# First load in one piece, and the last sixteen rows in five pieces: a row-wise ReLU sum

## The chip, the cores and the metric

The kernel runs on one core of one Trainium2 chip. The metric is device time in microseconds (us) for one execution; the time before is the median of three runs. The profile is one execution recorded by the hardware profiler, and its own time, the span, is somewhat shorter than the run time, because it starts with the first recorded instruction and ends with the last.

## The reference

```python
def setup_inputs():
    batch, seq, dim = 32, 512, 1024
    return {"x": np.random.randn(batch, seq, dim).astype(np.float32)}

def reference(x: np.ndarray) -> np.ndarray:
    relu_x = np.maximum(x, 0)
    return np.sum(relu_x, axis=-1).astype(np.float32)
```

There are 32 x 512 = 16384 rows of 1024 fp32 numbers, 64 MB (67.1 million bytes) in all. Each row gives one number: the sum of its positive elements. The output is 64 KB.

## The kernel before

**Rows on partitions.** Each of the 128 partitions handles J = 128 rows. `REGIONS = [1, 111, 16]` (line 8) cuts the input, in order of address, into three blocks. In the first block partition p holds one row, so that the block is 512 KB of consecutive memory; in the second it holds 111 consecutive rows (neighbouring partitions start 444 KB apart); in the third it holds 16 (64 KB apart). `xv` and `ov` (lines 45 to 49) are the views of input and output by block.

**Staging.** `buf` is a ring of NB = 3 buffers of 16 rows for each partition. `CHUNKS` (line 9) lists seven chunks of 16 rows. Chunk 0 comes in two loads, the single row of the first block (4 KB for each partition) and 15 rows of the second block (60 KB); chunks 1 to 6 are one load each of 64 KB for each partition. All loads go through SyncE's queue (SP), issued in the loop of line 85; chunk c waits until VectorE (DVE) has finished chunk c - 3 (line 87). Both loads of chunk 0 are moved in the instruction list ahead of SP's arrival at the start barrier (lines 79 to 84 and 95 to 97).

**The two engines.** For chunks 0 to 5 (`NTWO` of them, loop of line 138), ScalarE (ACT) does the ReLU in place over several rows at once (line 145), DVE sums the rows of each step (line 160), and in the later chunks some rows are done whole by one engine. "Whole" means one instruction that does ReLU and sum: `on_act` (line 127), which the profile shows as ACTIVATE and a read of the accumulator, or `on_dve` (line 130), shown as TENSOR_SCALAR_CACHE_REDUCE and a read of the accumulator. For chunk 6 and everything behind it, rows go alternately to DVE and ACT, whole (lines 173 to 185). `res` holds the results, one column for each of a partition's 128 rows.

**The transposed store.** The results of the first block lie in column 0 of `res`, one number for each partition. DVE transposes 32 columns of `res` in 32 x 32 squares after chunk 1 (lines 167 to 169), so that four partitions of `turned` hold the 128 numbers, and SP stores these four runs of 128 bytes (line 117), behind the last loads in its queue.

**The last 16 rows.** They come in seven loads: `TAIL = [8, 4, 2]` whole rows (line 101), and the last two rows, seen as one run of 2048 elements, in four pieces: elements 0 to 912 (`first`), 1536 to 2048 (`second`), 1280 to 1536 (`third`), in that order (line 112), and last 912 to 1280 into the tile `seam` (line 115). This last piece lies across the border of the two rows. Each earlier piece gives a partial sum (`first` two, one on each engine), which is written into `seam` right beside the loaded elements: two numbers ahead of them and two behind. Then ACT sums the 114 numbers that belong to the second-last row, and DVE the 258 of the last row (lines 199 to 203). The partial sums are not negative, so a ReLU over them changes nothing. `s_half` and `s_seam` count the partial sums and the load; `s_last` counts the two final sums.

**The stores.** The results of the second block are stored (line 123) when both engines have finished chunk 6 and the load of `third` has landed; those of the third block (line 207) after `s_last`. The program ends when the stores have landed.

Of the kernel before, what the change touches and what calls it, by code (L numbers as in the profile page):

```python
# [3 lines left out]
P = 128  # L4
D = 1024
BIG = 16
NB = 3
REGIONS = [1, 111, 16]
CHUNKS = [[(0, 0, 1), (1, 0, 15)]] + [[(1, 16 * c + 15, 16)] for c in range(6)]
ACT_STEPS = [[16], [7, 9], [7, 9], [7, 9], [4, 5, 7], [3, 4, 5]]  # L10
DVE_STEPS = [[4, 5, 7], [7, 4, 5], [7, 4, 5], [7, 4, 5], [4, 5, 7], [3, 4, 5]]
TAIL = [8, 4, 2]
CUT = 912
HEAD = 256


def bass_relu_sum_kernel(
    nc: bass.Bass,
    x: bass.AP,
    out: bass.AP,  # L20
):

    fp32 = mybir.dt.float32
    ALU = mybir.AluOpType
    AF = mybir.ActivationFunctionType
    X = mybir.AxisListType.X

    B, S, _ = x.shape
    J = B * S // P
    NBIG = len(CHUNKS)
    assert BIG * NBIG + sum(TAIL) + 2 == J == sum(REGIONS)  # L40

    xr = x.rearrange("b s d -> (b s) d")
    of = out.rearrange("b s -> (b s)")
    start = [sum(REGIONS[:i]) for i in range(len(REGIONS))]
    xv = [
        xr[P * s : P * (s + n), :].rearrange("(p j) d -> p j d", p=P)
        for s, n in zip(start, REGIONS)
    ]
    ov = [of[P * s : P * (s + n)].rearrange("(p j) -> p j", p=P) for s, n in zip(start, REGIONS)]

    buf = nc.alloc_sbuf_tensor("buf", [P, NB, BIG, D], fp32)
    w = D - CUT
    seam = nc.alloc_sbuf_tensor("seam", [P, 2 + w + HEAD + 2], fp32)
    res = nc.alloc_sbuf_tensor("res", [P, J], fp32)
    turned = nc.alloc_sbuf_tensor("turned", [P, 32], fp32)

    n_in = NBIG + len(TAIL) + 3
    s_in = [nc.alloc_semaphore(f"s_in{i}") for i in range(n_in)]
    s_act = nc.alloc_semaphore("s_act")
    s_dve = nc.alloc_semaphore("s_dve")  # L60
    s_fact = nc.alloc_semaphore("s_fact")
    s_fdve = nc.alloc_semaphore("s_fdve")
    s_half = nc.alloc_semaphore("s_half")
    s_seam = nc.alloc_semaphore("s_seam")
    s_last = nc.alloc_semaphore("s_last")
    s_turn = nc.alloc_semaphore("s_turn")
    s_store = nc.alloc_semaphore("s_store")
    s_out = nc.alloc_semaphore("s_out")

    sp, act, dve = nc.sync, nc.scalar, nc.vector  # L70

    NTWO = len(ACT_STEPS)
    done = [sum(map(len, DVE_STEPS[: c + 1])) for c in range(NTWO)]


    tb = NBIG % NB


    code = nc.main_func.blocks[0].instructions
    arrival = next(  # L80
        i
        for i, ins in enumerate(code)
        if ins.engine == mybir.EngineType.SP and type(ins).__name__ == "InstDrain"
    )
    for c in range(NBIG + 1):
        if c >= NB:
            sp.wait_ge(s_dve, done[c - NB])
        if c < NBIG:
            i = 0
            for g, j, n in CHUNKS[c]:  # L90
                sp.dma_start(  # L91
                    out=buf[:, c % NB, i : i + n, :], in_=xv[g][:, j : j + n, :]
                ).then_inc(s_in[c], 16)
                i += n
                if c == 0:
                    code.insert(arrival, code.pop())
                    arrival += 1
    r = 0
    tail = []
    for i, n in enumerate(TAIL):  # L100
        sp.dma_start(out=buf[:, tb, r : r + n, :], in_=xv[-1][:, r : r + n, :]).then_inc(  # L101
            s_in[NBIG + i], 16
        )
        tail.append((r, n, s_in[NBIG + i]))
        r += n


    rows = xv[-1].rearrange("p j d -> p (j d)")[:, r * D : (r + 2) * D]
    flat = buf[:, tb, r : r + 2, :].rearrange("p j d -> p (j d)")
    first, second, third = [(0, CUT), (D + D // 2, 2 * D), (D + HEAD, D + D // 2)]  # L110
    for k, (lo, hi) in enumerate((first, second, third)):
        sp.dma_start(out=flat[:, lo:hi], in_=rows[:, lo:hi]).then_inc(  # L112
            s_in[NBIG + len(TAIL) + k], 16
        )
    sp.dma_start(out=seam[:, 2 : 2 + w + HEAD], in_=rows[:, CUT : D + HEAD]).then_inc(s_seam, 16)
    sp.wait_ge(s_turn, 1)
    sp.dma_start(
        out=of[0:P].rearrange("(k q) -> k q", q=32), in_=turned[0:P:32, 0:32]
    ).then_inc(s_store, 16)
    sp.wait_ge(s_fact, 1)  # L120
    sp.wait_ge(s_fdve, 1)
    sp.wait_ge(s_in[-1], 16)
    sp.dma_start(out=ov[1][:, :], in_=res[:, start[1] : start[2]]).then_inc(s_store, 16)


    def on_act(t, acc):
        return act.activation(t, t, AF.Relu, accum_out=acc)  # L127

    def on_dve(t, acc):
        return dve.tensor_scalar(  # L130
            out=t, in0=t, scalar1=0.0, scalar2=None, op0=ALU.max, op1=ALU.add, accum_out=acc
        )

    def row(c, i):
        return buf[:, c % NB, i, :], res[:, c * BIG + i : c * BIG + i + 1]

    k = 0
    for c in range(NTWO):
        alone = BIG - sum(ACT_STEPS[c])
        act.wait_ge(s_in[c], 16 * len(CHUNKS[c]))  # L140
        r = 0
        ready = []
        for n in ACT_STEPS[c]:
            t = buf[:, c % NB, r : r + n, :]
            act.activation(t, t, AF.Relu).then_inc(s_act, 1)  # L145
            k += 1
            ready += [k] * n
            r += n
        for i in range(BIG - alone // 2, BIG):
            on_act(*row(c, i))  # L150
        if alone:
            dve.wait_ge(s_in[c], 16 * len(CHUNKS[c]))
            for i in range(BIG - alone, BIG - alone // 2):
                on_dve(*row(c, i))
        r = seen = 0
        for n in DVE_STEPS[c]:
            if ready[r + n - 1] > seen:
                seen = ready[r + n - 1]
                dve.wait_ge(s_act, seen)
            dve.tensor_reduce(  # L160
                out=res[:, c * BIG + r : c * BIG + r + n],
                in_=buf[:, c % NB, r : r + n, :],
                axis=X,
                op=ALU.add,
            ).then_inc(s_dve, 1)
            r += n
        if c == 1:
            dve.wait_ge(s_dve, done[c])
            dve.transpose(out=turned[:, :], in_=res[:, 0:32]).then_inc(s_turn, 1)  # L169


    j0 = NBIG * BIG
    for c in range(NTWO, NBIG):
        act.wait_ge(s_in[c], 16 * len(CHUNKS[c]))
        dve.wait_ge(s_in[c], 16 * len(CHUNKS[c]))
        for i in range(BIG):
            ins = (on_act if i % 2 else on_dve)(*row(c, i))
            if i >= BIG - 2:
                ins.then_inc(s_fact if i % 2 else s_fdve, 1)
    for r, n, s in tail:  # L180
        act.wait_ge(s, 16)
        dve.wait_ge(s, 16)
        for i in range(r, r + n):
            f = on_act if (i - r) % 2 else on_dve
            f(buf[:, tb, i, :], res[:, j0 + i : j0 + i + 1])

    lo, hi = first
    act.wait_ge(s_in[-3], 16)
    dve.wait_ge(s_in[-3], 16)
    on_act(flat[:, lo : CUT // 2], seam[:, 0:1]).then_inc(s_half, 1)  # L190
    on_dve(flat[:, CUT // 2 : hi], seam[:, 1:2]).then_inc(s_half, 1)
    k = 2 + w
    lo, hi = second
    act.wait_ge(s_in[-2], 16)
    on_act(flat[:, lo:hi], seam[:, k + HEAD : k + HEAD + 1]).then_inc(s_seam, 1)
    lo, hi = third
    dve.wait_ge(s_in[-1], 16)
    on_dve(flat[:, lo:hi], seam[:, k + HEAD + 1 : k + HEAD + 2]).then_inc(s_seam, 1)
    act.wait_ge(s_seam, 16 + 2)
    act.wait_ge(s_half, 2)  # L200
    on_act(seam[:, 0:k], res[:, J - 2 : J - 1]).then_inc(s_last, 1)
    dve.wait_ge(s_seam, 16 + 2)
    on_dve(seam[:, k : k + HEAD + 2], res[:, J - 1 : J]).then_inc(s_last, 1)


    sp.wait_ge(s_last, 2)
    sp.dma_start(out=ov[-1][:, :], in_=res[:, start[-1] : J]).then_inc(s_out, 16)
    sp.wait_ge(s_store, 16 * (len(REGIONS) - 1))
    sp.wait_ge(s_out, 16)


# [26 lines left out]
```

## Time and profile before

| | us |
|---|---|
| median of three runs | 160.8 (160.77 to 160.82) |
| span of the profiled execution | 159.4 |
| DVE busy | 120.6 |
| ACT busy | 101.5 |
| landing of chunk 0 (the wait of ACT before its first ReLU ends) | 21.61 |
| DVE starts its first sum | 35.50 |
| both engines start chunk 6 | 137.72 |
| the final sums over `seam` start | 157.47 |
| the last store is issued | 157.93 |

The times below the first four rows are starts in the timeline, counted from the start of the span. In the profile, "SPq" is SyncE issuing to the DMA queue, and the time from issue to landing of a load includes all the loads that wait ahead of it in the same queue. The trace also holds a record of each packet that a DMA engine moved, with start, duration and size; in this kernel one packet is the run of one partition in one load, so a load has 128 of them, eight on each of 16 DMA engines.

### The profile page before, as it was taken

To read this page: it belongs to the slowest core of one execution; us is meant where nothing else is said; L and a number is where in the kernel's file an instruction comes from. 1 tells how busy PE (TensorE), PEld (TensorE's weight loads), DVE (VectorE), ACT (ScalarE), POOL (GpSimd) and SP (SyncE) were. 2 spreads that over 40 slices of the span, in tenths; PEclk is the share of its full clock that TensorE was granted. 3 is DMA by queue.
4 is the path that set the end of the run, shared out by engine and by line. 5 is a ranking of instruction groups with operands and counts; after the bars stand their busy time and mean duration, and the time that the engine had idled before them with its cause. 6 is when DMAs were issued, how large, how long until landed. Compare 5 with 4: busy or idle time off the path is not lost.

```text
span 159.4 us, 150 instructions
## 1 busy us (share of the span) xinstructions
DVE 120.6 (76%) x59; ACT 101.5 (64%) x54; POOL 0.2 (0%) x4
## 2 busy tenths in 40 slices
DVE  0000000009999999999999999999999999898995
ACT  3000059980799708996099941999329980496975
POOL 0000000000000000000000000000000000000000
DMA  9997996996996997989979969969969979798994
GB/s 378 493 401 339 493 526 263 526 526 263 526 493 296 526 444 345 526 378 411 526 312 477 526 263 526 526 263 526 526 263 526 444 345 526 321 469 374 417 400 142
DMA packets 2457, 67.18 MB, mean 421 GB/s; under 512 B 536, under 2 KB 792, under 8 KB 1176
## 3 DMA queue, kind: packets, MB, share of 16 engines
q1 hardware_dynamic: 2456, 67.18, 98.1%
q14 instruction: 1, 0.01, 0.0%
HBM read 67.11 MB, written 0.07 MB: 421 GB/s over the span
## 4 chain that ended last, share of the span: by engine, by line
DVE 55%; DMA 34%; ACT 9%; SPq 2%; issue 0%
DVE res L160 54%; DMA buf<-in_x_dram 34%; ACT buf L145 9%; SPq L101 1%; SPq L112 1%; DVE buf L130 0%; DVE seam L130 0%; SPq L91 0%; DVE turned L169 0%
## 5 line engine op out<-in xcount | busy, mean ns | idle before, releaser
L160 DVE TENSOR_REDUCE res<-buf 128x4 f32<-128x4096 f32 (+3 forms) x18 | 99.4, 5596 | 35.5 <-ACT buf L145 35.5
L145 ACT ACTIVATE buf<-buf 128x7168 f32<-128x7168 f32 (+5 forms) x13 | 80.4, 6233 | 46.1 <-DMA buf<-in_x_dram 46.1
L127 ACT ACTIVATE buf<-buf 128x1024 f32<-128x1024 f32 (+2 forms) x19 | 19.0, 999 | 8.9 <-DMA buf<-in_x_dram 8.9
L130 DVE TENSOR_SCALAR_CACHE_REDUCE buf<-buf 128x1024 f32<-128x1024 f32 (+2 forms) x19 | 20.7, 1143 | 1.7 <-DMA buf<-in_x_dram 1.6
L127 ACT ACTIVATION_READ_ACCUMULATOR buf<-buf 128x1 f32 x19 | 3.6, 188 | 0.0
L145 ACT ACT_TABLE_LOAD x1 | 1.3, 1283 | 1.3 <-PEq L223 1.3
L130 DVE DVE_READ_ACCUMULATOR buf<-buf 128x1 f32 x19 | 1.6, 84 | 0.0
L130 DVE TENSOR_SCALAR_CACHE_REDUCE seam<-seam 128x258 f32<-128x258 f32 x1 | 0.4, 421 | 0.0
L127 ACT ACTIVATE seam<-seam 128x114 f32<-128x114 f32 x1 | 0.3, 300 | 0.1
L169 DVE STREAM_TRANSPOSE turned<-res 128x32 f32<-128x32 f32 x1 | 0.2, 211 | 0.0
L127 ACT ACTIVATION_READ_ACCUMULATOR seam<-seam 128x1 f32 x1 | 0.2, 186 | 0.0
L223 POOL MEMSET const-bfloat16-1.0<- 128x1 bf16 x1 | 0.1, 101 | 0.0
L223 POOL MEMSET const-uint8-127<- 128x1 uint8 x1 | 0.1, 101 | 0.0
L223 POOL MEMSET const-float32-0.0<- 128x1 f32 x1 | 0.1, 98 | 0.2 <-issue 0.2
L223 POOL MEMSET const-float32-1.0<- 128x1 f32 x1 | 0.1, 98 | 0.0
L130 DVE DVE_READ_ACCUMULATOR seam<-seam 128x1 f32 x1 | 0.1, 82 | 0.0
## 6 DMA issues: line engine op xcount, KB each, us to landing
buf<-in_x_dram SPq DMA_DIRECT2D x1, 7680.0 KB, 21.1
buf<-in_x_dram SPq DMA_DIRECT2D x1, 4096.0 KB, 25.3
buf<-in_x_dram SPq DMA_DIRECT2D x1, 2048.0 KB, 29.9
buf<-in_x_dram SPq DMA_DIRECT2D x1, 1024.0 KB, 31.9
buf<-in_x_dram SPq DMA_DIRECT2D x1, 512.0 KB, 3.3
buf<-in_x_dram SPq DMA_DIRECT2D x1, 456.0 KB, 32.5
buf<-in_x_dram SPq DMA_DIRECT2D x1, 256.0 KB, 32.7
seam<-in_x_dram SPq DMA_DIRECT2D x1, 184.0 KB, 32.6
```

What stands on the lines that cost most here:

```text
L101: sp.dma_start(out=buf[:, tb, r : r + n, :], in_=xv[-1][:, r : r + n, :]).then_inc(s_in[NBIG + i], 16)
L112: sp.dma_start(out=flat[:, lo:hi], in_=rows[:, lo:hi]).then_inc(s_in[NBIG + len(TAIL) + k], 16)
L127: return act.activation(t, t, AF.Relu, accum_out=acc)
L130: return dve.tensor_scalar(out=t, in0=t, scalar1=0.0, scalar2=None, op0=ALU.max, op1=ALU.add, accum_out=acc)
L145: act.activation(t, t, AF.Relu).then_inc(s_act, 1)
L160: dve.tensor_reduce(out=res[:, c * BIG + r : c * BIG + r + n], in_=buf[:, c % NB, r : r + n, :], axis=X, op=ALU.add,).then_inc(s_dve, 1)
L169: dve.transpose(out=turned[:, :], in_=res[:, 0:32]).then_inc(s_turn, 1)
L223: nc = _bacc.Bacc("TRN2", target_bir_lowering=False, num_devices=1)
```

## The change

`ROWS = [112, 16]` replaces the three blocks by two: partition p holds 112 consecutive rows of the first block (448 KB from partition to partition) and, as before, 16 of the last. All seven chunks are single loads of 64 KB for each partition, and one load, instead of two, is moved ahead of SP's arrival at the start barrier. The transpose on DVE, the tile `turned` and its store are gone; one store of 112 columns replaces the stores of 1 and of 111.

The last 16 rows come in loads of 9 and 4 rows, and the last three rows, seen as one run of 3072 elements, in three pieces: 0 to 1884, 2304 to 3072, and last 1884 to 2304 into `seam`. The first piece is a whole row (DVE, straight into `res`) and 860 elements of the second-last row (ACT, a partial sum). The second piece, 768 elements of the last row, is split 432 to ACT and 336 to DVE, one partial sum each. `seam` then holds one partial sum, 420 loaded elements and two partial sums; ACT sums the 165 numbers of the second-last row, DVE the 258 of the last. Of the nine rows ACT takes five and DVE four (before, each took four of eight).

```diff
-REGIONS = [1, 111, 16]
-CHUNKS = [[(0, 0, 1), (1, 0, 15)]] + [[(1, 16 * c + 15, 16)] for c in range(6)]
+ROWS = [112, 16]
-TAIL = [8, 4, 2]
-CUT = 912
-HEAD = 256
+TAIL = [9, 4]
+ENDS = [1884, 2304]
+SPLIT = 432
...
-    w = D - CUT
-    seam = nc.alloc_sbuf_tensor("seam", [P, 2 + w + HEAD + 2], fp32)
+    lo, hi = ENDS
+    w = hi - lo
+    seam = nc.alloc_sbuf_tensor("seam", [P, 1 + w + 2], fp32)
     res = nc.alloc_sbuf_tensor("res", [P, J], fp32)
-    turned = nc.alloc_sbuf_tensor("turned", [P, 32], fp32)
...
         if c < NBIG:
-            i = 0
-            for g, j, n in CHUNKS[c]:
-                sp.dma_start(
-                    out=buf[:, c % NB, i : i + n, :], in_=xv[g][:, j : j + n, :]
-                ).then_inc(s_in[c], 16)
-                i += n
-                if c == 0:
-                    code.insert(arrival, code.pop())
-                    arrival += 1
+            sp.dma_start(
+                out=buf[:, c % NB, :, :], in_=xv[0][:, BIG * c : BIG * (c + 1), :]
+            ).then_inc(s_in[c], 16)
+            if c == 0:
+                code.insert(arrival, code.pop())
...
-    rows = xv[-1].rearrange("p j d -> p (j d)")[:, r * D : (r + 2) * D]
-    flat = buf[:, tb, r : r + 2, :].rearrange("p j d -> p (j d)")
-    first, second, third = [(0, CUT), (D + D // 2, 2 * D), (D + HEAD, D + D // 2)]
-    for k, (lo, hi) in enumerate((first, second, third)):
-        sp.dma_start(out=flat[:, lo:hi], in_=rows[:, lo:hi]).then_inc(
+    rows = xv[-1].rearrange("p j d -> p (j d)")[:, r * D : (r + 3) * D]
+    flat = buf[:, tb, r : r + 3, :].rearrange("p j d -> p (j d)")
+    for k, (f, t) in enumerate(((0, lo), (hi, 3 * D))):
+        sp.dma_start(out=flat[:, f:t], in_=rows[:, f:t]).then_inc(
             s_in[NBIG + len(TAIL) + k], 16
         )
-    sp.dma_start(out=seam[:, 2 : 2 + w + HEAD], in_=rows[:, CUT : D + HEAD]).then_inc(s_seam, 16)
-    sp.wait_ge(s_turn, 1)
-    sp.dma_start(
-        out=of[0:P].rearrange("(k q) -> k q", q=32), in_=turned[0:P:32, 0:32]
-    ).then_inc(s_store, 16)
+    sp.dma_start(out=seam[:, 1 : 1 + w], in_=rows[:, lo:hi]).then_inc(s_seam, 16)
     sp.wait_ge(s_fact, 1)
     sp.wait_ge(s_fdve, 1)
     sp.wait_ge(s_in[-1], 16)
-    sp.dma_start(out=ov[1][:, :], in_=res[:, start[1] : start[2]]).then_inc(s_store, 16)
+    sp.dma_start(out=ov[0][:, :], in_=res[:, 0 : start[1]]).then_inc(s_store, 16)
...
-        if c == 1:
-            dve.wait_ge(s_dve, done[c])
-            dve.transpose(out=turned[:, :], in_=res[:, 0:32]).then_inc(s_turn, 1)
...
         for i in range(r, r + n):
-            f = on_act if (i - r) % 2 else on_dve
+            f = on_dve if (i - r) % 2 else on_act
             f(buf[:, tb, i, :], res[:, j0 + i : j0 + i + 1])
-    lo, hi = first
-    act.wait_ge(s_in[-3], 16)
-    dve.wait_ge(s_in[-3], 16)
-    on_act(flat[:, lo : CUT // 2], seam[:, 0:1]).then_inc(s_half, 1)
-    on_dve(flat[:, CUT // 2 : hi], seam[:, 1:2]).then_inc(s_half, 1)
-    k = 2 + w
-    lo, hi = second
     act.wait_ge(s_in[-2], 16)
-    on_act(flat[:, lo:hi], seam[:, k + HEAD : k + HEAD + 1]).then_inc(s_seam, 1)
-    lo, hi = third
+    dve.wait_ge(s_in[-2], 16)
+    on_dve(flat[:, 0:D], res[:, J - 3 : J - 2])
+    on_act(flat[:, D:lo], seam[:, 0:1]).then_inc(s_seam, 1)
+    act.wait_ge(s_in[-1], 16)
     dve.wait_ge(s_in[-1], 16)
-    on_dve(flat[:, lo:hi], seam[:, k + HEAD + 1 : k + HEAD + 2]).then_inc(s_seam, 1)
-    act.wait_ge(s_seam, 16 + 2)
-    act.wait_ge(s_half, 2)
-    on_act(seam[:, 0:k], res[:, J - 2 : J - 1]).then_inc(s_last, 1)
-    dve.wait_ge(s_seam, 16 + 2)
-    on_dve(seam[:, k : k + HEAD + 2], res[:, J - 1 : J]).then_inc(s_last, 1)
+    on_act(flat[:, hi : hi + SPLIT], seam[:, 1 + w : 2 + w]).then_inc(s_seam, 1)
+    on_dve(flat[:, hi + SPLIT : 3 * D], seam[:, 2 + w : 3 + w]).then_inc(s_seam, 1)
+    cut = 1 + 2 * D - lo
+    act.wait_ge(s_seam, 16 + 3)
+    on_act(seam[:, 0:cut], res[:, J - 2 : J - 1]).then_inc(s_last, 1)
+    dve.wait_ge(s_seam, 16 + 3)
+    on_dve(seam[:, cut : 3 + w], res[:, J - 1 : J]).then_inc(s_last, 1)
```

## The prediction

> **What bounds the kernel now.** I read the page first: the DMA rows, then the groups by form, then the waits, then the timeline of both ends.
>
> ```profile
> span 159.4 us, 150 instructions
> ...
> DMA  9997996996996997989979969969969979798994
> ...
> q1 hardware_dynamic: 2456, 67.18, 98.1%
> ```
>
> The data queue's packets occupy the 16 DMA engines for 98.1% of the span. In the packet records a 64 KB packet takes 2418 ns at least, and the means of chunks 1 to 6 are 2420 to 2427 ns, back to back. So the queue is full from its first packet (1.01 us) to the last load's landing.
>
> ```profile
> DVE res L160 <- ACT buf L145: 35.5, 1, 35.5
> ACT buf L127 <- DMA buf<-in_x_dram: 8.9, 4, 6.7
> DVE buf L130 <- DMA buf<-in_x_dram: 1.6, 4, 0.5
> ```
>
> In the waits (total, times, longest), DVE waits for ACT only at the start and later four times for loads, never over 0.5 us: it is the second bound, close behind the queue. The chain of waits names DVE for 55% only because DVE works without a gap between 35.50 and 137.3; it then still waits 0.42 us for chunk 6.
>
> ```profile
> 156.65 0.63 ACT L127 ACTIVATE buf<-buf 128x512 f32<-128x512 f32 x1
> 157.01 0.42 DVE L130 TENSOR_SCALAR_CACHE_REDUCE buf<-buf 128x256 f32<-128x256 f32 x1 [0.40 <-DMA buf<-in_x_dram]
> 157.08 0.34 SPq L123 DMA_DIRECT2D out_dram<-res  x1
> 157.19 0.19 ACT L127 ACTIVATION_READ_ACCUMULATOR buf<-buf 128x1 f32 x1
> 157.36 0.08 DVE L130 DVE_READ_ACCUMULATOR buf<-buf 128x1 f32 x1
> 157.47 0.30 ACT L127 ACTIVATE seam<-seam 128x114 f32<-128x114 f32 x1
> 157.47 0.42 DVE L130 TENSOR_SCALAR_CACHE_REDUCE seam<-seam 128x258 f32<-128x258 f32 x1
> 157.68 0.19 ACT L127 ACTIVATION_READ_ACCUMULATOR seam<-seam 128x1 f32 x1
> 157.82 0.08 DVE L130 DVE_READ_ACCUMULATOR seam<-seam 128x1 f32 x1
> 157.93 0.34 SPq L207 DMA_DIRECT2D out_dram<-res  x1
> ```
>
> At the end (start, duration) the last partial sum is read out at 157.44, and `seam` lands at 157.44 too: queue and engines finish together. From the last store's issue (157.93) to the end of the span it is 1.46 us, and the run's median lies 1.4 us above the span; I carry both over unchanged.
>
> **The cost of one load more.** Packet minima by size: 64 KB 2418 ns, 32 KB 1213, so (2418 - 1213) / 32 = 37.66 ns for each KB and a constant of 8 ns; 4 KB by this line is 159, as measured. Each load adds eight such constants on an engine and a semaphore record of 9 ns: 0.07 us.
>
> **Head: one load instead of two.** 8 x (159 + 2268 - 2418) + 9 ns = 0.08 us less on each DMA engine. The issue-to-data time is 1.01 us for the first load, and I take the same for 64 KB, since later issues of 64 KB loads took 0.33 us on SP against 0.39 for this one.
>
> ```profile
> buf<-in_x_dram SPq DMA_DIRECT2D x1, 7680.0 KB, 21.1
> ...
> buf<-in_x_dram SPq DMA_DIRECT2D x1, 512.0 KB, 3.3
> ```
>
> How the queue runs up is the unknown. In the records the 4 KB packets average 198 ns over 159, eight of them 0.31 us; 0.20 of it is each engine's first packet (620 ns on four engines, 355 on four, near 230 on the others), 0.11 is later packets of up to 338. The 60 KB packets average 2289 over 2267, eight of them 0.17 us. One load must still pay the first packet. If the other 0.11 + 0.17 go with the split, the head gains 0.28 more; if the first two 64 KB packets of each engine are as slow as the slow 60 KB ones (2479, 0.21 over), it loses 0.42. I take zero between them: the excess comes with all engines starting together, which stays, and the zero lies between the two rows. Head: -0.08, bounds -0.36 and +0.34.
>
> **The chunks.** Chunks 1 to 6 are the same 64 KB packets, now from places 448 KB apart instead of 444. The nearest row is the last block, whose partitions are 64 KB apart in both kernels, also a multiple of 64 KB: its 32 KB packets all took 1213 ns, on the line above. So I take zero; bounds: zero, and all chunks as slow as the slowest now (2427.5 against 2420: 7.5 ns x 56 packets = 0.42). A gain has no room, 2420 being 2 ns above the minimum. The Trainium skill, "DMA: Bandwidth & Descriptors", section "Latency and other measured facts", lists copies whose row pitch is a large power of two as slower (207 GB/s at 512 KiB, 214 when padded by 4 KiB); 448 KiB is seven times a power of two where 444 is not near one, so it speaks against this change. The last block's 64 KB pitch at full rate does not show such a loss here; by the rule's ratio the sum would be about +4.5 us, an estimate.
>
> **The transpose and its store.** DVE loses 0.21 us (L169) and the wait before it. It lies in the gapless stretch that ends in the 0.42 us wait for chunk 6, so it only lengthens that wait: zero. Without this cover it would be worth 0.23. The store of 4 packets of 128 bytes (13 ns each, landing among the last loads) is zero too; SP is past it at 126, with 31 us of waiting ahead. SP's issues earlier by this change meet a full queue. The one store of 448 instead of 444 bytes per partition is issued at the landing of the second piece, about 0.2 us sooner than now, and is done before the last store.
>
> **Tail, the loads.** From the landings of the trace: 8 rows 147.41, 4 rows 4.89 later, then 2 rows +2.51, first +1.12, second +0.69, third +0.36, seam +0.45. After: 9 rows need 8 x 150.6 ns = 1.20 more, 148.62; 4 rows 153.50; 7536 bytes +2.32 (2.51 less 8 x 656 bytes by the line), 155.82; 3072 bytes +0.97 (between 3648 bytes, 1.12, and 2048, 0.69), 156.79; 1680 bytes +0.51, 157.29. That is 0.15 before the present landing, two loads' constants.
>
> **Tail, the engines.** In the timeline a whole row takes ACT 1.04 us from start to start, DVE 1.14 (the first 0.02 more), and the end of the accumulator read is 0.10 (ACT) and 0.08 (DVE) behind that. Shorter forms on ACT: 114 elements 0.30, 456 0.58, 512 0.63, 1024 1.04, so 0.81 ns an element: 860 elements 0.91, 432 0.57, 165 0.34. On DVE 256 take 0.42, 456 0.62: 336 take 0.50.
> ACT: start 148.64, five rows to 153.86 (the four rows are there since 153.50), two rows to 155.94 (the first piece is there since 155.82), 860 elements to 156.85 (second piece 156.79), 432 elements, read out at 157.51.
> DVE: four rows to 153.21, waits to 153.52, two rows to 155.81, one row from 155.84 to 156.99, 336 elements, read out at 157.50.
> So both are 0.2 later than `seam` at 157.29, and the final sums start at 157.54, not 157.47. DVE's 258 elements end 0.50 later as now, 157.97; ACT's 165 at 157.98 (0.10 behind 0.34); the store is issued at 158.01 against 157.93. Tail: +0.08: the 0.15 that the queue gains is not used, because the last four instructions of each engine are back to back. If the engines kept up it would be -0.15; if each of ACT's four steps lost another 0.03 to its wait, +0.2.
>
> **Sum.** Head -0.08, chunks 0, transpose 0, tail +0.08: zero. Span 159.4, run 160.8. A shift of the head moves every landing, so it is passed on to the end in full.
>
> **Rivals.**
> 1. *Faster: the run-up gets smooth.* The 0.28 goes with the split and the head gives -0.36: -0.28, 160.5; with the engines keeping up in the tail as well, -0.51, 160.3. For it: later 4 KB packets of up to 338 ns and 60 KB ones of 2479, both absent in chunk 2 (mean 2420). Against: all engines still start within 0.4 us.
> 2. *Slower: the 448 KB step makes the chunks collide.* Place: the packets of all seven chunks; price: 56 packets x the excess; it decides from 0.32 / 56 = 6 ns a packet. At 7.5 ns +0.42, 161.2; at 12 ns +0.67, 161.5. For it: chunk 6 shows that packets of 2427 occur. Against: the last block's packets.
> 3. *Slower: the run-up gets worse.* Two slow packets for each engine instead of the present 0.28: +0.34 in the head, with the tail +0.42, 161.2. For it: without the 512 KB of consecutive memory, all engines begin on rows 448 KB apart; the slow 60 KB packets are of that kind.
> 4. *Much slower: every packet of the chunks is slow.* If all 64 KB packets ran like the slowest one of now (2513 ns, in chunk 1, the minimum being 2418), 95 ns x 56 = +5.3 us, 166.1. No row of the last block is like it. The skill's rule on pitches, named above, would act in this way.
>
> **How the numbers follow.** A measurement of this kernel tells about 0.2%, 0.32 us, from no change. No change 0.42 (160.8, own range 160.5 to 161.1); rival 1 0.22; rival 2 0.20; rival 3 0.12; rival 4 0.04. Rival 1 is the chance of faster, 2 to 4 together, 0.36, of slower. The range goes from rival 1's lower time, 160.3, to rival 2's upper, 161.5, which leaves out rival 4 and the outer parts of 1 and 2.
>
> **What would show it.** Right: chunk 0 lands near 21.5 and chunk 6 near 137.6; the packet means of the chunks stay at 2420 to 2427; `seam` lands near 157.2 and the final sums start 0.2 later, behind ACT's 432 elements; DVE's wait for chunk 6 grows from 0.42 to about 0.6. Wrong: chunk 0 landing before 21.3 or after 21.9 (rivals 1 and 3); landings of successive chunks more than 19.40 apart (now 19.35; rival 2); the final sums waiting for `seam` instead of ACT, so that the engines have slack I did not see.

## The result, and the profile after

The changed kernel takes 161.18 us (median of 22 runs, 161.10 to 161.43) against 160.85 of the kernel before (22 runs beside it). The ratio is 1.0019, 95% interval 1.0013 to 1.0025: slower by 0.33 us, clear of noise, where no change was forecast.

The loss has two parts, and the first split comes from the runs alone, since each lists its span beside its time. The time around the span, run time less span, is 1.52 after the change (mean of 22 runs, with a scatter of 0.03), so the 161.18 stands for a span of 159.66; the mean of the listed spans is 159.69. The kernel before has 1.36 around the span in the 5 sets of runs beside the experiments below (1.35 to 1.38), so its 160.85 stands for a span of 159.49. That is +0.17 in the span and +0.16 around it, a part of the run that no line of the profile shows.

The page of the changed kernel, its first line and the data queue:

```profile
span 159.7 us, 142 instructions
...
q1 hardware_dynamic: 2016, 67.18, 97.9%
```

The queue is nearly as full as before (98.1%). The waits of the two engines (total us, times, longest), and the two ends of the timeline (start, duration):

```profile
ACT buf L133 <- DMA buf<-in_x_dram: 46.8, 6, 19.8
DVE res L148 <- ACT buf L133: 35.8, 1, 35.8
ACT buf L115 <- DMA buf<-in_x_dram: 9.1, 2, 6.6
DVE buf L118 <- DMA buf<-in_x_dram: 2.6, 3, 1.7
```

```profile
21.91 13.86 ACT L133 ACTIVATE buf<-buf 128x16384 f32<-128x16384 f32 x1 [19.84 <-DMA buf<-in_x_dram]
35.79 9.81 DVE L148 TENSOR_REDUCE res<-buf 128x4 f32<-128x4096 f32 x2 [35.79 <-ACT buf L133]
```

```profile
138.00 1.22 DVE L118 TENSOR_SCALAR_CACHE_REDUCE buf<-buf 128x1024 f32<-128x1024 f32 x1 [0.62 <-DMA buf<-in_x_dram]
...
157.11 0.55 ACT L115 ACTIVATE buf<-buf 128x432 f32<-128x432 f32 x1
157.14 0.35 SPq L111 DMA_DIRECT2D out_dram<-res  x1
157.24 0.08 DVE L118 DVE_READ_ACCUMULATOR buf<-buf 128x1 f32 x1
157.24 0.50 DVE L118 TENSOR_SCALAR_CACHE_REDUCE buf<-buf 128x336 f32<-128x336 f32 x1
157.56 0.19 ACT L115 ACTIVATION_READ_ACCUMULATOR buf<-buf 128x1 f32 x1
157.66 0.08 DVE L118 DVE_READ_ACCUMULATOR buf<-buf 128x1 f32 x1
157.78 0.34 ACT L115 ACTIVATE seam<-seam 128x165 f32<-128x165 f32 x1
157.78 0.42 DVE L118 TENSOR_SCALAR_CACHE_REDUCE seam<-seam 128x258 f32<-128x258 f32 x1
...
158.24 0.34 SPq L190 DMA_DIRECT2D out_dram<-res  x1
```

The timeline of the kernel before has these two starts in the same places:

```profile
21.61 13.86 ACT L145 ACTIVATE buf<-buf 128x16384 f32<-128x16384 f32 x1 [19.06 <-DMA buf<-in_x_dram]
...
137.72 1.22 DVE L130 TENSOR_SCALAR_CACHE_REDUCE buf<-buf 128x1024 f32<-128x1024 f32 x1 [0.42 <-DMA buf<-in_x_dram]
```

In this execution everything is late from the first landing on: ACT's first ReLU starts at 21.91 (before 21.61), chunk 6 is there at 138.00 (137.72), the last store is issued at 158.24 (157.93). From the landing of chunk 6 to the last store it is 20.26 against 20.23. So the loss inside the span lies ahead of 21.9 us, and the packet records show it there: the first sixteen 64 KB packets, one on each DMA engine, take 3112 ns in the mean (2834 to 3385), and all that follow in this chunk 2418 to 2420. `seam` lands at 157.59 and the engines are ready 0.19 later, as the back-to-back starts of ACT and DVE show.

The chain of waits names it differently, since both engines now hold the end:

```profile
0.00 21.88 DMA buf<-in_x_dram
...
35.79 86.34 DVE res L148 x15
122.13 0.02 issue
122.15 26.75 DMA buf<-in_x_dram
148.89 0.02 issue
148.92 8.84 ACT buf L115 x18
157.76 0.02 issue
157.78 0.43 ACT seam L115 x2
```

ACT works without a gap from the landing of the nine rows (148.92) to the final sum.

### The profile page after: what moved, and what is told of

It is laid out like the page before. It is cut to its first block, busy times and chain, and to the rows that moved or that the text cites. A ratio compares the mean times of both kernels' runs of the same rounds, so it can differ in the third digit from the quotient of the medians.

```text
span 159.7 us, 142 instructions
## 1 busy us (share of the span) xinstructions
DVE 119.8 (75%) x56; ACT 101.4 (64%) x54; POOL 0.2 (0%) x4
## 4 chain that ended last, share of the span: by engine, by line
DVE 54%; DMA 30%; ACT 14%; issue 0%
DVE res L148 54%; DMA buf<-in_x_dram 30%; ACT buf L133 9%; ACT buf L115 6%; ACT seam L115 0%
## 5 line engine op out<-in xcount | busy, mean ns | idle before, releaser
L118 DVE TENSOR_SCALAR_CACHE_REDUCE buf<-buf 128x1024 f32<-128x1024 f32 (+1 forms) x18 | 20.1, 1176 | 2.6 <-DMA buf<-in_x_dram 2.6
```

The costliest lines, as they stand in the source:

```text
L118: return dve.tensor_scalar(out=t, in0=t, scalar1=0.0, scalar2=None, op0=ALU.max, op1=ALU.add, accum_out=acc)
```

## The experiments

Two measures serve throughout: the landing of chunk 0, as the mean over the 16 DMA engines or for the last of them, which is the one that ACT waits for (one profiled execution each), and, from all runs of a kernel, the mean span and the mean time around it.

### Which part of the change: four kernels

**e1**, the kernel before with blocks 112 and 16, the first load still split:

```diff
-REGIONS = [1, 111, 16]
-CHUNKS = [[(0, 0, 1), (1, 0, 15)]] + [[(1, 16 * c + 15, 16)] for c in range(6)]
+REGIONS = [112, 16]
+CHUNKS = [[(0, 0, 1), (0, 1, 15)]] + [[(0, 16 * c, 16)] for c in range(1, 7)]
...
-            dve.transpose(out=turned[:, :], in_=res[:, 0:32]).then_inc(s_turn, 1)
```

> The kernel before with row blocks 112 and 16: chunk 0 still comes as 1 and 15 rows, but both from the 112-row block (448 KB from partition to partition), and there is no transpose and no separate store; the tail is that of before. Theories for the 0.30 us that chunk 0 lands later after the change (21.88 against 21.59): T1, the size of the first packets: a first packet of 64 KB makes the run-up longer (mean 3116 ns of the first sixteen against 2418) than one of 4 KB. T2, the step: at 448 KB, a multiple of 64 KB, the engines run in phase at the start. T3, the start barrier: with one load ahead of it instead of two it is passed 0.48 us earlier, and the activation table load and the next issue fall into the run-up. T1 and T3: chunk 0 lands at 21.6 (within 0.1), 160.85 us, ratio 1.000. T2: chunk 0 at 21.85 or later, ratio 1.002.

**e2**, the kernel before with the single row at the end of chunk 6, so that chunk 0 is one load at a step of 444 KB:

```diff
-REGIONS = [1, 111, 16]
-CHUNKS = [[(0, 0, 1), (1, 0, 15)]] + [[(1, 16 * c + 15, 16)] for c in range(6)]
+REGIONS = [111, 1, 16]
+CHUNKS = [[(0, 16 * c, 16)] for c in range(6)] + [[(0, 96, 15), (1, 0, 1)]]
...
+    dve.transpose(out=turned[:, :], in_=res[:, 80:112]).then_inc(s_turn, 1)
```

> The kernel before with the blocks in the order 111, 1, 16: chunk 0 is one load of 64 KB for each partition, 444 KB apart; the single row is the last of chunk 6 (so chunk 6 has two loads), and its results are transposed and stored after chunk 6. The tail is that of before. T1 and T3: chunk 0 lands at 21.85 to 21.9, first packets near 3100 ns, chunk 6 at 138.0 to 138.05, 161.1 to 161.2 us, ratio 1.002. T2: chunk 0 at 21.5, ratio 0.9995 to 1.0005.

**e3**, the kernel after with two loads ahead of the start barrier:

```diff
-            if c == 0:
+            if c <= 1:
                 code.insert(arrival, code.pop())
+                arrival += 1
```

> The kernel after the change, with the load of chunk 1 also moved ahead of SP's arrival at the start barrier, so that the barrier is passed and the activation table loaded as late as before the change. T1 and T2: chunk 0 lands at 21.85 to 21.9, 161.18 us, ratio 1.002. T3: chunk 0 lands at 21.6, 160.9 us, ratio 1.0003.

**e4**, the kernel after with the blocks, the two first loads and the transposed store of before, so the five-piece tail alone:

```diff
-ROWS = [112, 16]
+ROWS = [1, 111, 16]
+CHUNKS = [[(0, 0, 1), (1, 0, 15)]] + [[(1, 16 * c + 15, 16)] for c in range(6)]
...
+            dve.transpose(out=turned[:, :], in_=res[:, 0:32]).then_inc(s_turn, 1)
```

> The head of before (row blocks 1, 111 and 16, two first loads, transposed store) with the five-piece tail of the change. All theories: chunk 0 at 21.6; seam lands 0.13 earlier than before (157.31), the final sums start 0.03 to 0.08 later (157.50 to 157.55) behind ACT's 432 elements; ratio 1.000 to 1.0005. If the five pieces were to blame for part of the loss, the ratio would be 1.001 or more.

| | ratio (95%) | span | around | chunk 0, last engine | chunk 0, mean | first 16 packets, ns |
|---|---|---|---|---|---|---|
| before (21 runs beside) | 1 | 159.47 | 1.36 | 21.59 | 21.34 | 362 (4 KB) |
| e1 | 1.0048 (1.0035 to 1.0060) | 159.68 | 1.90 | 21.81 | 21.59 | 603 (4 KB) |
| e2 | 1.0042 (1.0029 to 1.0054) | 160.12 | 1.36 | 22.06 | 21.57 | 3144 (64 KB) |
| e3 | 1.0024 (1.0015 to 1.0033) | 159.69 | 1.52 | 21.83 | 21.55 | 3128 (64 KB) |
| e4 | 1.0025 (1.0016 to 1.0034) | 159.61 | 1.60 | 21.68 | 21.44 | 345 (4 KB) |

T3 falls: with the barrier as late as before, e3 is the kernel after again. The other three don't fit any theory in their times. For e1 and e4 the column "around" says why: it takes values from 1.36 to 1.90, which no theory had named. e4, meant to cost nothing, is 0.25% slower, of which 0.24 us lies around the span. e2's part around the span is that of before; its loss is all in the span, where besides the late chunk 0 it has one load more in chunk 6. So from here there were two questions. For the run-up the four kernels leave T1 and T2 both wanting: a late chunk 0 in e1 (4 KB packets at 448 KB) speaks against size alone, one in e2 (64 KB at 444) against the step alone.

### The part around the span

The trace gave the first hint: a fetch of 8 KB of instructions, which the page shows as a queue of its own when it falls inside the span. The kernel before has it at 159.21, inside the span, while SP waits for the last store. In the packet records e4 has one at 160.97, 1.4 us after the end of its span, and e1 two, at 161.26 and 161.31. Waits that are long satisfied add instructions without adding work; two of them become one instruction in these programs:

```diff
+    for _ in range(8):
+        sp.wait_ge(s_in[0], 16)
     sp.wait_ge(s_fact, 1)
```

is **e5** (kernel after), four instructions more on SP; **e6** has three more on DVE, **e7** is e4 with two more on SP.

> The kernel after the change with eight waits more on SP, all satisfied long before, between the last load's issue and the waits for the first store (four instructions more: SP has 22 in the program, as before the change; after it, 18). The runs so far show two parts of the 0.33 us: the spans grow by 0.22 (mean 159.69 over 22 runs against 159.47 of the kernel before), and the time around the span grows from 1.36 to 1.52. Theory A: the part around the span hangs on the number of SP's instructions (where the trace's fetch of 8 KB of instructions falls: at 159.2 inside the span before the change, at 160.97 and 161.26 in the two experiments with 20 and 21 instructions on SP, which have 1.60 and 1.90 around the span). Theory B: it hangs on DVE's number (41 and 42 with 1.36; 40 with 1.60 and 1.90; 39 with 1.52). A: 1.36 around the span, 161.0 to 161.05 us, ratio 1.0013, and a fetch inside the span near 159.5. B: 1.52, 161.2 us. The span stays at 159.7 by both.

> The kernel after the change with six satisfied waits (three instructions) more on DVE behind the sums of chunk 5, where it later waits 0.6 us for chunk 6: 42 instructions on DVE, 18 on SP. A (see the run with the waits on SP): 1.52 around the span, 161.2 us, ratio 1.0024. B: 1.36, 161.0 to 161.05 us. Span 159.7 by both.

> The run with the head of before and the five-piece tail, with four satisfied waits (two instructions) more on SP, which then has 22. A: 1.36 around the span instead of 1.60, 160.97 us, ratio 1.001. B: 1.60, 161.2 us, ratio 1.0025. The span is the second look at the tail alone: 159.50 if the tail costs 0.03 as the trace of the first run has it from chunk 6 to the last store (20.267 against 20.232), 159.61 if the first run's mean span is its true cost. Chunk 0 should land at 21.6 to 21.7, mean over the 16 engines 21.35 to 21.45.

Both theories fell: e5 has 1.50 around the span, e6 1.52, e7 1.60 as e4 has. The fetch of e6 even lies inside its span, at 160.05 of 160.18, and this gains nothing. **e11** makes the numbers on SP, ACT and DVE together those of the kernel before (SP's eight waits are those of e5):

```diff
...
+    for _ in range(4):
+        dve.wait_ge(s_in[0], 16)
+    for _ in range(2):
+        act.wait_ge(s_in[0], 16)
     j0 = NBIG * BIG
```

> The kernel after the change with satisfied waits added on three engines, so that the numbers of instructions are those of the kernel before: SP 22, ACT 37, DVE 41 (they were 18, 36 and 39). The time around the span was 1.36 only in the two kernels with 37 on ACT and 41 or more on DVE, 1.50 to 1.60 in all with 36 on ACT, and 1.90 with 37 and 40. C, the numbers of instructions set the part around the span: 1.36 here, 161.0 to 161.05 us, ratio 1.0012. D, something else in the two programs does (the semaphores used, the last instructions): 1.50 to 1.52, 161.2 us. Span 159.7 by both.

It got worse, 1.73, with two late fetches (160.93 and 161.24): C in this form fell too, but the part did move with nothing changed except satisfied waits. The numbers had been counted in the program, where a sum on DVE is one instruction; in the trace it is two, with the read of the accumulator. So counted, DVE has 61 before, 58 after, and only 60 in e11. (ACT's numbers stay those of the program; the trace has 20 more on ACT in every kernel here.) **e12** adds three on DVE and one on ACT to the kernel after, **e13** one on ACT alone, and **e15** brings e4 to the counts of the kernel before.

> The kernel after the change with six satisfied waits (three instructions) more on DVE and two (one instruction) more on ACT. Counted with the accumulator reads in the trace, DVE then has 61 instructions of the program (before the change 61, after it 58, in the run with all counts of the program made equal 60), ACT 37 (before 37, after 36). C2, the place of each engine's last instructions relative to a block of fetched instructions sets the part around the span: 1.36, a fetch inside the span, 161.05 us, ratio 1.0012. D, something else: 1.50 or more, 161.2 us. The span stays at 159.7.

> The kernel after the change with two satisfied waits (one instruction) more on ACT only: ACT 37, DVE 58. If ACT's count alone sets the 0.16 around the span, 1.36 and 161.05 us; if it takes both (C2), 1.5 or more, 161.2 us.

> The head of before with the five-piece tail, with four satisfied waits (two instructions) more on DVE and two (one instruction) on ACT: DVE 61, ACT 37. C2: 1.36 around the span instead of 1.60; with the span of 159.50 to 159.60 that the two earlier runs of this head and tail had, 160.86 to 160.96 us, ratio 1.0002 to 1.0008: the five pieces by themselves cost 0.03 to 0.1. D: 1.50 or more, 161.1 us.

| DVE, ACT | kernels | around the span, us |
|---|---|---|
| 58, 36 | after; e3, e5, e8, e9, e10, e14, e16 | 1.50 to 1.53 |
| 59, 36 | e4, e7 | 1.60 |
| 61, 36 | e6 | 1.52 |
| 58, 37 | e13 | 1.85 |
| 60, 37 | e1, e11, e18 | 1.73 to 1.90 |
| 61, 37 | before; e12, e15 | 1.35 to 1.38 |
| 62, 37 | e2, e17 | 1.36 |

C2's number for the part around the span holds. e12 is the changed kernel with four instructions that do nothing, and this part is 1.365 (11 runs, 1.32 to 1.40) instead of 1.515. After, e6, e13 and e12 form a square: three instructions more on DVE alone leave 1.52, one more on ACT alone gives 1.85, both together 1.36. In e12's run time little of the gain is seen: 161.10, ratio 1.0017 (1.0008 to 1.0025), where C2 wanted 1.0012, because its spans are 0.10 longer in the mean, 159.79 against 159.69. The kernel before differs by 0.06 in this way between two of its sets of runs (159.47 beside e1 to e4, 159.53 beside e12), so part of it can be scatter between sets. The run time does show it in e15, which is e4 with three instructions more: 1.372 around the span instead of 1.60, and a time of 160.91, ratio 1.0002 (0.9993 to 1.0010), where e4 had 161.21. So the tail alone costs nothing that can be measured. e15's page has the fetch inside its span, as the page before had:

```profile
span 159.6 us, 148 instructions
...
q14 instruction: 1, 0.01, 0.0%
```

That the numbers of instructions on DVE and ACT set 0.15 to 0.5 us is shown; that late fetches are how they do it is not. In the profiled executions the two go together only in part. Where a fetch falls between 0.33 us ahead of the span's end and 0.10 behind it, 1.35 to 1.37 lie around the span (e2, e12, e15, e17), but 1.52 in e6. Without a fetch near the end it is 1.45 to 1.52. With one fetch more than 1.3 us late it is 1.51 (e4) and 1.66 (e7), with two 1.75 to 1.86 (e1, e11, e18). The Trainium skill, "Runtime: NRT & Kernel Launch", section "Instruction fetch mechanics", says that an engine's instructions come in blocks, fetched ahead, and that crossing into the next block is mostly hidden (it gives 16 KiB for a block; the fetches in these traces are of 8 KB). A fetch that lengthens the run would be one that is not hidden: e1, e7, e11 and e18 would fit that, e4 and e6 do not, and no run here settles it.

### The run-up

**e8**, the kernel after with its first 16 rows from 8 MB of consecutive memory:

```diff
-ROWS = [112, 16]
+ROWS = [16, 96, 16]
```

> The kernel after the change with row blocks 16, 96 and 16: chunk 0 is still one load of 64 KB for each partition, but its partitions lie 64 KB apart, so that it reads 8 MB of consecutive memory (its 16 columns are stored by one more DMA behind the last loads). The mean landing of chunk 0 over the 16 engines was 21.34 and 21.44 in the two runs that began with 512 KB of consecutive memory, and 21.55 to 21.60 in all four that began 444 or 448 KB apart, with 4 KB packets (21.59) as with 64 KB packets. Theory F: the cost comes from first reads at places far apart, not from the size of the packets (T1) and not from 448 against 444 (T2): mean landing 21.35 to 21.45 here, span 159.5 to 159.6. T1, size: 21.55 to 21.60, span 159.7. T2, phase at multiples of 64 KB: 21.55 or later.

Chunk 0 lands at 21.56 in the mean and the first packets take 3083 ns: F, first reads at places far apart, falls for 64 KB packets. T1's number is met, and so is T2's (21.55 or later), against which e2 speaks. (Its span of 159.98 contains one store more.) **e9** and **e10** put a load of 64 bytes for each partition ahead of all others in the kernel after:

```diff
+    sp.dma_start(out=warm[:, :], in_=xv[0][:, 0, 0:16]).then_inc(s_warm, 16)
```

(e10: `in_=xr[0:2, :].rearrange("r (q d) -> (r q) d", d=16)`.)

> The kernel after the change with one small load ahead of all others: 64 bytes at the start of each partition's first row (448 KB apart) into a scratch tile that nothing reads. It adds a load, 0.07 us or a little more on the queue. The first sixteen 64 KB packets took 3112 ns in the mean after the change (2418 is the minimum). W, first touch of a place: the small load pays it for all 128 places, the first 64 KB packets take 2420 to 2500, chunk 0 lands at 21.35 to 21.5 in the mean over the engines and the span falls to 159.5. R, run-up of each engine: the first packet of an engine is slow wherever it reads; the same numbers as W. S, sixteen long packets at once are slow at the start whatever went before: 3050 to 3150 as now, chunk 0 mean at 21.65, span 159.75.

> As the run before, but the 64 bytes for each partition come from 8 KB of consecutive memory (the first two rows of the input), so that only partition 0's place is touched ahead of its load. W: the first 64 KB packets stay at 3050 to 3150, chunk 0 mean at 21.65, span 159.75. R: 2420 to 2500, chunk 0 mean 21.35 to 21.5, span 159.5. S: 3050 to 3150.

The first 64 KB packets took 3158 and 3120 ns: a touch of the same places or of others changes nothing, so W and R fall and S, sixteen long packets at once, stands. The times were worse than any theory had: chunk 0 at 22.09 and 22.25 in the mean, ratios 1.0057 and 1.0067. The records say why: in e9 the small packets run from 0.99 to 1.43, and the 4-byte records that close their load on each engine end at 1.21 in the mean, but the 64 KB packets, whose load SP issued at 0.43, start only at 1.48 (mean 1.69). From issue to first packet it is 0.98 to 1.03 us for the first load of every kernel here and 1.05 for this second one, and 64 bytes are too short to cover it. The engines thus stood idle for about 0.5 us between the touch and the long packets; that a run-up comes back after such a pause is not excluded. In the kernel before, the 4 KB packets of the first load cover it (1.01 to 2.94). The start of the timeline of e9:

```profile
0.00 0.38 SPq L84 DMA_DIRECT2D warm<-in_x_dram  x1
...
0.43 1.63 SPq L91 DMA_DIRECT2D buf<-in_x_dram  x3
...
22.30 13.86 ACT L139 ACTIVATE buf<-buf 128x16384 f32<-128x16384 f32 x1 [19.75 <-DMA buf<-in_x_dram]
```

If size were all, 16 KB packets should lie between. **e14** (blocks 4, 108, 16, first load of 4 rows), **e16** (2, 110, 16, first load of 2 rows), both with the five-piece tail; **e18** is e1 with the first load of 4 rows, **e17** is e2 with the first load split into 1 and 15 rows. e17's edit against e2:

```diff
-CHUNKS = [[(0, 16 * c, 16)] for c in range(6)] + [[(0, 96, 15), (1, 0, 1)]]
+CHUNKS = [[(0, 0, 1), (0, 1, 15)]] + [[(0, 16 * c, 16)] for c in range(1, 6)] + [[(0, 96, 15), (1, 0, 1)]]
```

> Row blocks 4, 108 and 16 with the five-piece tail: chunk 0 comes as 4 rows (16 KB packets from 2 MB of consecutive memory) and 12 rows (48 KB packets). The excess over the minimum packet times in chunk 0, for each engine, was 0.42 to 0.51 us with 4 KB packets from 512 KB of consecutive memory, 0.60 with 4 KB packets 448 KB apart, 0.62 to 0.75 with 64 KB packets wherever they came from. S, the size of the first packets: between, 0.55 to 0.65, mean landing of chunk 0 21.45 to 21.5, span 159.55 to 159.65. N, nearness alone: 0.42 to 0.51, mean landing 21.3 to 21.45, span 159.5.

> Row blocks 2, 110 and 16 with the five-piece tail: the first packets are 8 KB from 1 MB of consecutive memory, 8 KB from partition to partition (so that the engines, which take four partitions each in a row, begin 32 KB apart; 16 KB with the single row, 64 KB in the run with 16 KB packets, 1792 KB at a step of 448). Ph, the engines collide where their places lie in step by multiples of 64 KB: two phases here, mean landing of chunk 0 21.5 to 21.7. N, only the nearness of the first 128 places counts (512 KB good, 2 MB bad): 21.4 to 21.6.

> The run with a single first load at 444 KB, with chunk 0 split into 1 and 15 rows of the same block: first packets of 4 KB, 444 KB apart (engines 1776 KB apart, which is 48 KB past a multiple of 64 KB). Ph: the mean landing of chunk 0 is 21.3 to 21.45 as with the 512 KB block. N: 21.55 to 21.6 as with 4 KB packets at 448.

> Row blocks 112 and 16 with the tail of before, chunk 0 split into 4 and 12 rows of the same block: first packets of 16 KB, 448 KB apart. If the 21.89 of the 16 KB packets from 2 MB came of the packets' size (or of a step that is a multiple of 64 KB between engines, Ph): 21.8 to 21.9. If it came of the 2 MB block: 21.55 to 21.6.

| first packets | partitions apart | mean landing of chunk 0 | runs of the profile |
|---|---|---|---|
| 4 KB | 4 KB | 21.32 to 21.44 | before, e4, e7, e15 |
| 4 KB | 444 KB | 21.37 | e17 |
| 4 KB | 448 KB | 21.59 | e1 |
| 8 KB | 8 KB | 21.59 | e16 |
| 16 KB | 16 KB | 21.89 | e14 |
| 16 KB | 448 KB | 21.50 | e18 |
| 64 KB | 64 KB | 21.56 | e8 |
| 64 KB | 444 KB | 21.57 | e2 |
| 64 KB | 448 KB | 21.52 to 21.61 | after, e3, e5, e6, e11, e12, e13 |

S in its simple form, where only the size of the first packets counts, falls (16 KB from consecutive memory is the worst of all), and so does N, nearness (21.57 was wanted for e17). Ph, engines that begin in step by multiples of 64 KB, has e17 as it said (21.37) and e16, which N had too, but not e18, where 21.8 was wanted and 21.50 came; so the 21.89 of e14 points to its block of 2 MB rather than to packets of 16 KB. With one profiled execution in most rows and a scatter of 0.1 in the rows that have several, this is as far as it goes. Settled is that a first load of 64 KB packets lands 0.1 to 0.3 us later than one that begins with 4 KB packets from 512 KB of memory, wherever the 64 KB come from. The cleanest pair is e2 and e17, which differ in the split of the first load alone: 21.57 against 21.37, and mean spans of 160.12 against 159.60. At 448 KB the same split gains nothing (e1, 21.59), so the place of the first reads counts too. Why sixteen first reads of 64 KB take 0.6 to 0.7 us over the minimum, and why the shorter ones depend on their places, stays open.

No kernel tried beats the kernel before. e15 is its equal; e17 is next (160.92, 1.0008, interval 0.9998 to 1.0017), with a load more in chunk 6.

## Why the prediction was wrong, point by point

**The sum** was zero, 160.8 us, and the measured loss is 0.33. The range held the time and the loss is 0.2%, at the edge of the bound that the text had set, but the measurement tells it from nothing, and two terms failed.

**The head: the first term that was mis-sized.** The prediction gave -0.08 for one load less and took zero for the run-up, because "the excess comes with all engines starting together, which stays". It does not stay: the excess over the minimum packet times in chunk 0 is 0.42 to 0.57 us for each engine in the four runs with the head of before (0.49 in the kernel before itself), and 0.70 in the kernel after. The engines also start later, at 1.23 in the mean instead of 1.14, the last at 1.70 instead of 1.34. So the head, put at -0.08, came out at +0.30: that much later the last engine lands chunk 0 in the profiled pair. Why the first packets are slow stays open. Over all runs the span grows by about 0.2, most of it the head's, since the tail alone adds 0.01 and 0.02 in e15 and e7 (0.14 in e4, the same tail: so much can one set of runs differ). The bound of +0.34 had room for it. The choice between the bounds was at fault: the nearest row for a first packet of 64 KB was not the second load's packets but the first packets of the queue, 620 ns where 159 is the minimum, and nothing in the trace of before showed a long packet in that place. Seen from the result, that was a reason to take the slow end.

**Rival 3** had the place and nearly the time (161.2), with a chance of 0.12. Its mechanism was another: not two packets of each engine with 0.21 too much, but the first one with 0.69 (3112 against 2418) and none after it. The time was partly luck, since half of the loss lies around the span, which rival 3 did not have. And 21.88 stays just inside the bound that the prediction had set for chunk 0 (21.9), so its own sign of being wrong was not given.

**Around the span: the second term, not seen as one.** The prediction carried "1.4 us above the span" over unchanged. It is 1.36 before and 1.52 after, and four idle instructions bring it back to 1.37 in e12, though e12's run time fell by only 0.08. This was half of the loss, and the prediction had no rival for it: every operation that the edit removed was priced by its duration, none by the change in an engine's number of instructions.

**The chunks** were right: the packet means of chunks 1 to 6 are 2418 to 2423 ns (2420 to 2427 before) and the landings follow each other by 19.34 to 19.36, at a step of 448 KB as at 444. Rivals 2 and 4 fall. The loss that the Trainium skill, "DMA: Bandwidth & Descriptors", section "Latency and other measured facts", lists for copies at a pitch of 512 KiB and more does not show in these loads at 448 KB. (The full rate of 214 GB/s there is that of a 4 MiB pitch padded by 4 KiB.)

**The transpose** was right at zero: DVE's wait for chunk 6 grew from 0.42 to 0.62, as forecast.

**The tail** was right in its mechanism and a little dear: from chunk 6 to `seam` it is 19.61 against 19.74 (0.13 less, forecast 0.15), the engines are ready 0.19 after `seam` (0.25 by the forecast's starts), and chunk 6 to the last store costs 0.03, not 0.08. e15's last starts show the same hand-over, ACT's 432 elements and DVE's 336 back to back and then both final sums:

```profile
156.98 0.55 ACT L126 ACTIVATE buf<-buf 128x432 f32<-128x432 f32 x1
157.01 0.34 SPq L122 DMA_DIRECT2D out_dram<-res  x1
157.09 0.08 DVE L129 DVE_READ_ACCUMULATOR buf<-buf 128x1 f32 x1
157.09 0.50 DVE L129 TENSOR_SCALAR_CACHE_REDUCE buf<-buf 128x336 f32<-128x336 f32 x1
157.43 0.19 ACT L126 ACTIVATION_READ_ACCUMULATOR buf<-buf 128x1 f32 x1
157.51 0.08 DVE L129 DVE_READ_ACCUMULATOR buf<-buf 128x1 f32 x1
157.65 0.42 DVE L129 TENSOR_SCALAR_CACHE_REDUCE seam<-seam 128x258 f32<-128x258 f32 x1
157.65 0.34 ACT L126 ACTIVATE seam<-seam 128x165 f32<-128x165 f32 x1
```

## What to carry to other kernels

Compare run time less span first: where two kernels differ by a few tenths of a microsecond, that part can hold half of it, and here a few satisfied waits moved it either way, by 0.15 us down and 0.33 up. Judge the start of a full queue by the first packets of each engine, not by what the same packets cost later, and let the first load be long enough to cover the second one's way from issue to data. When a price lies between far bounds and the trace has never shown the operation in its new place, the middle is a guess: here the slow end came.

## What was not expected of the hardware

- The number of instructions on two engines changes the run time outside the span: 1.36 us with 61 on DVE and 37 on ACT, 1.52 with 58 and 36, 1.85 with 58 and 37 (six runs of e13, from 1.44 to 2.03).
- Sixteen first packets of 64 KB take 3034 to 3158 ns in eleven profiles, whether 64, 444 or 448 KB apart and whether a small load went ahead; the packets behind them in chunk 0 take 2418 to 2424 in the mean.
- In e16, which stores two columns, 8 bytes for each partition, the end is held up: the last store lands 3.6 us after its issue where 1.4 is usual, though its packets have all run by 159.23 of a span of 161.8. The page of e16 (KB each, us to landing):

```profile
out_dram<-res SPq DMA_DIRECT2D x1, 55.0 KB, 4.5
out_dram<-res SPq DMA_DIRECT2D x1, 1.0 KB, 34.3
out_dram<-res SPq DMA_DIRECT2D x1, 8.0 KB, 3.6
```

With 16 bytes for each partition (e14, which differs from e16 in its block sizes alone) the last store took its usual 1.4. That the narrow store is the cause rests on this one comparison. All four runs of e16 have spans of 161.3 to 162.1, and so its ratio, 1.0147, says nothing of its head.
